# The up-projection of two MLPs by one level of Strassen's algorithm, in a two-block sequence model on one core

## The chip, the cores and the metric

The kernel runs on one core of one Trainium2 chip. The metric is the device time of the whole program in microseconds (us), and the figure compared is the median over runs. PE is TensorE's matmul, PEld its weight load, DVE VectorE, ACT ScalarE, POOL GpSimd and SP SyncE.

## The reference

Two layers of a hybrid block are followed by one layer of another block and a final norm, all float32, for 512 tokens of 1024 channels. The change touches only the MLP at the end of each first-block layer:

```python
def hybrid_layer(x, positions, norm_mix, w_in, conv_w, w_conv_out, ret_norm, w_ret_out, w_o,
                 norm_mlp, w_up, w_down):
    ...
    x = x + merged @ w_o
    h2 = rmsnorm(x, norm_mlp)
    return x + jnp.square(jax.nn.relu(h2 @ w_up)) @ w_down
```

`w_up` is 1024 x 4096 and `w_down` 4096 x 1024. The convolution, retention and gates ahead of `w_o`, and all of the second block (attention with selected and windowed keys, cross attention, gated MLP), keep their arithmetic.

## The kernel before

Activations lie channels by tokens: a tile has 128 channels on the partitions and 512 tokens, so `x` is eight tiles. Every float32 operand is written as the sum of two parts, hi and lo, that TensorE takes in one pass each, and a product is three matmuls: hi by hi, lo of the tokens by hi of the weights, hi of the tokens by lo of the weights (`mm3`, lines 233 to 235). An output tile of `w_up` or `w_o` is eight blocks of 128 x 128 weights, so 24 matmuls of 512 columns into one PSUM bank.

**The weight stream.** All weights lie in HBM as one array in the order of use. `_load` brings chunks of 16 blocks (1 MB, two buffers, SP queue). `_split` makes the parts of a unit of eight blocks: ACT rounds `raw` to `whi` (line 195), DVE subtracts to get `wlo` (line 196); three buffers of each. `block` hands out the next block and, at a unit's first block, asks for the split two units ahead.

**The order of the work.** A schedule written by hand sets the program order of every engine. `dense` runs the output tiles; the first G side by side up to a cut, so that late inputs are needed late. What follows an output tile (its evacuation) is a generator whose stages run at later ticks: `pulse` runs a stage of each once TensorE got `due` us of work since the last pulse, and then takes one step from the background list `bg`. `b1_norm_chain` puts two such steps there: the sum of squares over channels on PE (`norm_a`, line 340) with DVE and POOL making 1/rms of it (lines 343 and 345), and the broadcast over partitions (`bcast`, line 352) that ACT copies. Engines take their instructions in program order, each at its own pace.

**The MLP.** `ev_o` adds the output of `w_o` to `x` on DVE (line 561), makes the two parts of `x` times the norm's gain, and adds its squares to the running sum (`square_into`, ACT and, on POOL, line 363). The MLP is done in halves of 2048 hidden channels: 16 output tiles of `w_up`, each followed by relu (ACT), square (DVE), hi (ACT) and lo (DVE); then eight output tiles of `w_down` over 16 blocks each, scaled (DVE, line 589) and added to `x` (first half on POOL, line 594; second half on DVE, followed by the parts for the next layer).

```python
    def block(self, desc, n=1):
        ...
        self._split(u + AHEAD)
            a = [None] * 16
            ...
            self.dense(xm, [c8(f"w_up{i}", half * 2048, m) for m in range(16)], ev_up, G=1 if half else 2, cuts=[7])
            ...
            self.dense(a, [[(f"w_down{i}", half * 2048 + k * P, m * P) for k in range(16)] for m in range(KD)], ev_dn, G=2, cuts=[14])
```

Of the kernel before, what the change touches and what calls it, by code (L numbers as in the profile page):

```python
# [18 lines left out]
P = 128  # L19
S = 512  # L20
# [106 lines left out]
class Builder:  # L127
    def __init__(self, nc, tc, d, ccols, pcols, max_chunks):
        self.nc, self.tc, self.d = nc, tc, d
        self.ccols, self.pcols = ccols, pcols  # L130
        self.desc = []
        self.raw, self.whi, self.wlo = {}, {}, {}
        self.chunks = self.units = 0
        self.max_chunks = max_chunks
# [43 lines left out]
    def _load(self, c):  # L178
        while self.chunks <= min(c, self.max_chunks - 1):
            c0 = self.chunks  # L180
            t = self.wp.tile([P, CHUNK * P], F32, tag="raw", name=f"raw{c0}", bufs=2)
            self.nc.sync.dma_start(t, self.d["ws"][c0])
            self.raw[c0] = t
            self.chunks += 1

    def _split(self, u):
        last = self.max_chunks * (CHUNK // UNIT) - 1
        while self.units <= min(u, last):
            v = self.units
            c, h = divmod(v, CHUNK // UNIT)  # L190
            self._load(c + 2)
            raw = self.raw[c][:, h * UNIT * P:(h + 1) * UNIT * P]
            hi = self.wp.tile([P, UNIT * P], F32R, tag="whi", name=f"whi{v}", bufs=NW)
            lo = self.wp.tile([P, UNIT * P], F32R, tag="wlo", name=f"wlo{v}", bufs=NW)
            self.nc.scalar.activation(hi, raw, AF.Copy)  # L195
            self.nc.vector.tensor_sub(lo, raw, hi.bitcast(F32))  # L196
            self.whi[v], self.wlo[v] = hi, lo
            self.whi.pop(v - 8, None), self.wlo.pop(v - 8, None)
            self.units += 1

    def block(self, desc, n=1):
        """hi and lo of the next n blocks (adjacent in one unit); desc: one or a list."""
        ds = desc if n > 1 else [desc]
        i = len(self.desc)
        u, b = divmod(i, UNIT)
        assert b + n <= UNIT
        self._split(u + AHEAD)
        self.desc += ds
        return self.whi[u][:, b * P:(b + n) * P], self.wlo[u][:, b * P:(b + n) * P]

    def align(self):
        while len(self.desc) % UNIT:
# [1403 lines left out]
```

## Time and profile before

| | |
|---|---|
| runs, us | 2549.67, 2543.52, 2543.41 |
| median, us | 2543.52 |
| profiled execution, first to last instruction, us | 2547.5 |
| PE busy, us | 2523.5 (99%), 11,998 matmuls |
| weight load (PEld), us | 2102.5 (83%) |
| DVE, ACT, POOL busy, us | 1386.0 (54%), 911.7 (36%), 286.7 (11%) |
| mean granted clock | 0.994 |
| read from HBM | 232.15 MB, 92 GB/s |

No time of the profiled execution beside its span is on the page; the span lies between the runs. A matmul's duration holds its way through the array, and the next one starts before it ends: what a matmul costs in a stream is the distance between starts. Busy sums hold the same overlap.

### The profile page before, as it was taken

How to read it: one execution, taken by the hardware profiler on the slowest of the kernel's cores; microseconds unless marked ns; L12 is line 12 of the kernel's file. 1: busy time of each engine (PE TensorE's matmuls, PEld its weight loads, DVE VectorE, ACT ScalarE, POOL GpSimd, SP SyncE). 2: the span in 40 equal slices, each digit the busy share in tenths (PEclk: the TensorE clock that was granted, in tenths of full speed). 3: DMA queues.
4: the chain of work that ended last, by engine and by line, in shares of the span. 5: the costliest groups of instructions: out<-in, count | busy, mean ns of one | idle time of the engine just before them, and what ended most of it. 6: DMA issues, size and time to landing. Idle time of an engine off the chain costs nothing.

```text
span 2547.5 us, 29202 instructions
## 1 busy us (share of the span) xinstructions
PE 2523.5 (99%) x11998; PEld 2102.5 (83%) x11998; DVE 1386.0 (54%) x1902; ACT 911.7 (36%) x1416; POOL 286.7 (11%) x282
## 2 busy tenths in 40 slices
PE   8999999999999999999999999999999999999998
PEld 7888988888888888889888888888867888888886
DVE  6643645544344465356454434445679565683773
ACT  4232433333233322234333322333676444332221
POOL 2000100210100100011011000022100110220111
PEclk9999999999999999999999999999999999999999
DMA  4222222222222222222122222222200222222222
GB/s 177 107 99 100 73 77 86 97 99 100 100 91 94 97 100 99 100 83 83 68 98 99 99 99 87 96 98 103 102 32 34 101 84 96 85 100 100 99 85 81
DMA packets 34822, 236.13 MB, mean 93 GB/s; under 512 B 4032, under 2 KB 4032, under 8 KB 7040
## 3 DMA queue, kind: packets, MB, share of 16 engines
q1 hardware_dynamic: 33552, 231.90, 25.3%
q8 instruction: 94, 1.54, 0.2%
q0 software_dynamic: 416, 1.31, 0.2%
q10 hardware_dynamic: 720, 1.05, 0.1%
q14 instruction: 40, 0.33, 0.0%
HBM read 232.15 MB, written 2.10 MB: 92 GB/s over the span
## 4 chain that ended last, share of the span: by engine, by line
PE 96%; DVE 2%; ACT 1%; issue 1%; DMA 0%; POOL 0%; POOLq 0%; DVEq 0%; SPq 0%
PE mm L233 28%; PE mm L235 27%; PE mm L234 27%; PE nat L704 2%; PE nat L706 2%; PE nat L705 2%; PE oacc L1053 1%; PE ssq L340 1%; PE at L1042 1%; POOL ssq L363 0%; PE o L234 0%; PE o L235 0%; PE o L233 0%; PE bc L352 0%; DVE cv L228 0%
## 5 line engine op out<-in xcount | busy, mean ns | idle before, releaser
L233 PE MATMUL mm<-hi,whi 128*128 128x512 f32 x3040 | 1189.1, 391 | 6.9 <-ACT hi L225 6.9
L234 PE MATMUL mm<-lo,whi 128*128 128x512 f32 x3040 | 1184.8, 390 | 0.5 <-DVE lo L228 0.5
L235 PE MATMUL mm<-hi,wlo 128*128 128x512 f32 x3040 | 1184.8, 390 | 0.0
L196 DVE TENSOR_TENSOR wlo<-raw,whi 128x1024 fp32r<-128x1024 f32 x432 | 589.1, 1366 | 601.6 <-ACT whi L195 599.8
L233 PEld LDWEIGHTS mm<-hi,whi 128*128 128x128 f32 x3040 | 571.7, 188 | 123.7 <-ACT hi L225 6.9
L235 PEld LDWEIGHTS mm<-hi,wlo 128*128 128x128 f32 x3040 | 571.4, 188 | 119.3
L234 PEld LDWEIGHTS mm<-lo,whi 128*128 128x128 f32 x3040 | 571.7, 188 | 118.2 <-DVE lo L228 1.0
L195 ACT ACTIVATE whi<-raw 128x1024 fp32r<-128x1024 f32 x432 | 454.3, 1054 | 597.0 <-PE mm L234 541.2
L363 POOL TENSOR_TENSOR ssq<-ssq,sq 128x512 f32<-128x512 f32 x65 | 86.3, 1327 | 778.6 <-ACT sq L225 755.9
L225 ACT ACTIVATE up<-mm 128x512 f32<-128x512 f32 x64 | 38.0, 597 | 202.9 <-PE mm L235 202.9
L704 PE MATMUL nat<-whi,hi 128*128 128x256 f32 (+2 forms) x320 | 95.0, 297 | 0.0
L705 PE MATMUL nat<-wlo,hi 128*128 128x256 f32 (+2 forms) x320 | 94.2, 294 | 0.0
L706 PE MATMUL nat<-whi,lo 128*128 128x256 f32 (+2 forms) x320 | 94.2, 294 | 0.0
L225 ACT ACTIVATE hi<-x,par 128x512 fp32r<-128x512 f32 x48 | 34.1, 721 | 121.4 <-DVE x L561 47.1
L1479 POOL TENSOR_TENSOR fy<-fy,fy 128x512 f32<-128x512 f32 x22 | 44.6, 2028 | 250.9 <-DVE fy L228 242.5
L589 DVE TENSOR_TENSOR dn<-mm,rbc 128x512 f32<-128x512 f32 x32 | 22.1, 691 | 87.7 <-PE mm L235 87.7
L228 DVE SCALAR_TENSOR_TENSOR fy<-fz,par,fy 128x512 f32<-128x512 f32 x88 | 66.1, 752 | 6.1
L704 PEld LDWEIGHTS nat<-whi,hi 128*128 128x128 f32 x320 | 61.1, 191 | 1.4
L705 PEld LDWEIGHTS nat<-wlo,hi 128*128 128x128 f32 x320 | 61.1, 191 | 1.4
L706 PEld LDWEIGHTS nat<-whi,lo 128*128 128x128 f32 x320 | 61.1, 191 | 1.3
L628 POOL TENSOR_TENSOR ra<-ra,rb 128x512 f32<-128x512 f32 x16 | 27.5, 1721 | 291.6 <-DVE ra L627 281.3
L225 ACT ACTIVATE hi<-fy 128x512 fp32r<-128x512 f32 x22 | 13.9, 634 | 119.8 <-POOL fz L1468 107.5
(322 smaller groups left out, 2218.4 us busy)
## 6 DMA issues: line engine op xcount, KB each, us to landing
raw<-ws SPq DMA_DIRECT2D x215, 1024.0 KB, 4.8
x<-x SPq DMA_DIRECT2D x8, 256.0 KB, 5.6
raw<-ws SPq DMA_DIRECT2D x2, 512.0 KB, 5.2
dec<-dec SPq DMA_DIRECT2D x1, 1024.0 KB, 10.1
mem<-mem POOLq DMA_DIRECT2D x4, 256.0 KB, 4.6
y<-out ACTq DMA_DIRECT2D x4, 256.0 KB, 2.1
y<-out SPq DMA_DIRECT2D x4, 256.0 KB, 2.2
par<-par SPq DMA_DIRECT2D x1, 596.0 KB, 8.2
```

What stands on the lines that cost most here:

```text
L195: self.nc.scalar.activation(hi, raw, AF.Copy)
L196: self.nc.vector.tensor_sub(lo, raw, hi.bitcast(F32))
L225: self.nc.scalar.activation(out, in_, f, **kw)
L228: self.nc.vector.scalar_tensor_tensor(out, a, s, b, op0=op0, op1=op1, **kw)
L233: mm(out, w[0], x[0], start=start, stop=False, **kw)
L234: mm(out, w[0], x[1], start=False, stop=False, **kw)
L235: mm(out, w[1], x[0], start=False, stop=stop, **kw)
L363: self.nc.gpsimd.tensor_tensor(st["ssq"], st["ssq"], q, op=ALU.add)
L704: mm(p, xc[0], w[0][:, :n], start=k == 0, stop=False)
L705: mm(p, xc[0], w[1][:, :n], start=False, stop=False)
L706: mm(p, xc[1], w[0][:, :n], start=False, stop=k == K - 1)
L1479: nc.gpsimd.tensor_tensor(y, y, tmp["g"], op=ALU.mult)
```

## The change

**Products.** For two output tiles of `w_up` (a pair) the blocks are seen as four pairs of input tiles by two output tiles, and the tokens as two halves of 256. One level of Strassen's algorithm in Winograd's form makes the 2 x 2 x 2 product from seven products instead of eight. Each of the seven runs over four sums of weight blocks with 256 columns of token sums: 7 x 4 x 3 = 84 matmuls of 256 columns take the place of 48 of 512. They are numbered 1 to 7 in the code. Two PSUM banks per pair (`A`, `B`) hold sums that build up over the products, and copies of `A` between products take intermediate states to SBUF (`y1`, `y2`).

**Token sums.** `halves` makes, for each two tiles of `x`, four sums of 256 tokens on DVE and the hi and lo parts of seven operands: seven ACT and seven DVE instructions of 256 elements. It is a generator in four stages behind every second output tile of `w_o`.

**Weight sums.** Three of the seven weight operands (7, 5, 3) are a block row that a transfer loads plus one that a second transfer adds in place, issued from POOL (`accum_op`, 72 of these; 24 of 512 KB, 48 of 256 KB). Operands 6 and 3 get a further sum from a finished unit on DVE (`onto`: 24 of 1024 elements a partition, 16 of 512). 1 and 2 are plain.

**MLP in quarters.** A quarter is four pairs of `w_up` and then eight output tiles of `w_down` over eight blocks each. Pairs overlap: while the new pair runs products 1, 2, 7, 6, the old one runs 5, 3, 4. The first three quarters add into `x` on POOL, the last on DVE.

**Weight stream.** The unit of load is now the unit of split (up to 512 KB, six buffers); loads are asked for six units ahead, adding transfers four, splits two; four buffers of parts. There are 512 loads instead of 217 and 512 splits instead of 432.

How DVE's order moves at the start of the MLP of layer 0 (`x_91` and `x_94` are the last tile of `x`, `ms` the mean square from the sum of squares, `wlo` parts of weight units). Before:

```order
L561 TENSOR_TENSOR x_91<-mm_3973,x_91 128x512
L228 SCALAR_TENSOR_TENSOR lo_4004<-x_91,par,hi_4003 128x512
L196 TENSOR_TENSOR wlo_4014<-raw_3859,whi_4013 128x1024
L343 TENSOR_SCALAR ms_4047<-ssq_4042 128x4
L196 TENSOR_TENSOR wlo_4052<-raw_3859,whi_4051 128x1024
```

Now (`raw` added to `raw` is the further weight sum, `tu` and `tv` the token sums, `tf` the lo part of a token operand):

```order
L712 TENSOR_TENSOR x_94<-mm_4123,x_94 128x512
L224 TENSOR_TENSOR raw_3967<-raw_3967,raw_3928 128x512
L228 TENSOR_TENSOR wlo_4178<-raw_3967,whi_4177 128x512
L390 TENSOR_TENSOR tu_4199<-y_495_4165 128x256
L391 TENSOR_TENSOR tu_4199<-y_495_4165,y_496_4166 128x256
L392 TENSOR_TENSOR tv_4200<-tu_4199,y_495_4165 128x256
L393 TENSOR_TENSOR tv_4200<-tv_4200,y_496_4166 128x256
L498 TENSOR_SCALAR ms_4210<-ssq_4205 128x4
L228 TENSOR_TENSOR wlo_4218<-raw_4029,whi_4217 128x1024
L280 TENSOR_TENSOR tf_4230<-y_495_4165,tf_4230 128x256
```

`ms` stood behind one lo part and one weight unit; it now stands behind a weight sum, a weight unit and the four token sums, and the first token operand of the last two tiles behind `ms` and another weight unit. On PE the sum of squares stood 24 matmuls of 512 columns behind the last one of `w_o`; it now stands 18 matmuls of 256 columns behind it, and the broadcast another nine behind that.

How POOL's order moves where `w_down` ends and the next part of `w_up` begins, in layer 0 (`x` are tiles of the residual, `dn` a scaled output tile, `sq` squares). Before, first half to second half:

```order
L594 TENSOR_TENSOR x_83<-dn_4927,x_83 128x512
L594 TENSOR_TENSOR x_85<-dn_4989,x_85 128x512
L594 TENSOR_TENSOR x_89<-dn_5051,x_89 128x512
L594 TENSOR_TENSOR x_91<-dn_5113,x_91 128x512
L363 TENSOR_TENSOR ssq_5827<-ssq_5827,sq_5842 128x512
```

Now, first quarter to second quarter:

```order
L752 TENSOR_TENSOR x_84<-dn_4928,x_84 128x512
L213 DMA raw_4864<-wa 128x512
L752 TENSOR_TENSOR x_86<-dn_4963,x_86 128x512
L752 TENSOR_TENSOR x_92<-dn_4997,x_92 128x512
L752 TENSOR_TENSOR x_94<-dn_5031,x_94 128x512
L213 DMA raw_4967<-wa 128x1024
L213 DMA raw_5001<-wa 128x512
L213 DMA raw_5090<-wa 128x1024
```

The adding transfer of the unit that holds products 7 and 5 of the quarter's second step (`raw_4967`, 512 KB) stands behind the addition of the last output tile of `w_down`; nothing of POOL's was waited for there before.

The diff, cut to its core:

```diff
-CHUNK = 16
-AHEAD = 2
+H = S // 2
+LOAD, ACCUMULATE, SPLIT = 6, 4, 2
...
+    def sum_to(self, v):
...
+            more = self._known(u)["more"]
+            if more is not None:
+                at, n = more[0] * P, len(more[1]) * P
+                self.nc.gpsimd.dma_start(self.raw[u][:, at:at + n], self.d["wa"][self.more_at[u]][:, :n], accum_op=ALU.add)
...
+    def part_to(self, v):
...
+            if onto is not None:
+                self.nc.vector.tensor_tensor(raw[:, :n], raw[:, :n], self.raw[onto][:, :n], op=ALU.add)
...
+            self.nc.scalar.activation(hi[:, :n], raw[:, :n], AF.Copy)
+            self.nc.vector.tensor_sub(lo[:, :n], raw[:, :n], hi[:, :n].bitcast(F32))
...
+    def advance(self, u):
...
+        self.load_to(u + LOAD)
+        self.sum_to(u + ACCUMULATE)
+        self.part_to(u + SPLIT)
...
+    def halves(self, x1, x2, g1, g2):
...
+        self.act(y1, x1, AF.Copy, scale=g1)
+        self.act(y2, x2, AF.Copy, scale=g2)
+        yield
...
+        tt(u[:, :H], y1[:, :H], y1[:, H:], op=ALU.subtract)
+        tt(u[:, H:], y1[:, H:], y2[:, H:], op=ALU.subtract)
+        tt(v[:, :H], u[:, H:], y1[:, :H], op=ALU.subtract)
+        tt(v[:, H:], v[:, :H], y2[:, :H], op=ALU.add)
+        yield
...
+            self.act(out[f][:, :H], of[f])
+        yield
...
+            self.lo(out[f][:, H:], of[f], out[f][:, :H])
...
+    def strassen(self, X, pairs, done):
...
+            for k in ks or range(K):
+                w = slice((o + k) * P, (o + k + 1) * P)
+                while X[k] is None:
+                    self.tick(0.0)
+                self.mm3(p, (self.whi[u][:, w], self.wlo[u][:, w]), (X[k][f][:, :H], X[k][f][:, H:]),
+                         k == 0 and (f in (1, 2) or f == 4 and j in E), k == K - 1, skip_group_check=True)
+            self.tick(1.2)
...
+            xu = unit([(7, new), (5, old)])
+            yu = unit([(6, new), (3, old)], xu)
+            if old is not None:
+                unit([(4, old)])
+            if j == -1:
+                for f in (1, 2, 7):
+                    product(f, new, range(K - 1))
+                for f in (1, 2):
+                    product(f, new, [K - 1])
...
-            self.dense(xm, [c8(f"w_up{i}", half * 2048, m) for m in range(16)], ev_up, G=1 if half else 2, cuts=[7])
+            self.strassen(xm, [[c8(f"w_up{i}", (quarter * Q + 2 * j + e) * P, 0) for e in range(2)] for j in range(Q // 2)], up)
...
-            self.dense(a, [[(f"w_down{i}", half * 2048 + k * P, m * P) for k in range(16)] for m in range(KD)], ev_dn, G=2, cuts=[14])
+            self.dense(a, [[(f"w_down{i}", (quarter * Q + k) * P, m * P) for k in range(Q)] for m in range(KD)], ev_dn, G=3, cuts=[6])
...
-NW = 3
+NRAW = 6
+NW = 4
```

## Rows read from the trace of the kernel before

**Rows 1.** The page, parts 1 and 4: busy engines, and the chain that ended last

```profile
PE 2523.5 (99%) x11998; PEld 2102.5 (83%) x11998; DVE 1386.0 (54%) x1902; ACT 911.7 (36%) x1416; POOL 286.7 (11%) x282
...
PE 96%; DVE 2%; ACT 1%; issue 1%; DMA 0%; POOL 0%; POOLq 0%; DVEq 0%; SPq 0%
```

**Rows 2.** Stretches (MLP of layer 0, attention): busy us per engine (instructions), clock, DMA, GB/s

```profile
529.00:878.00 349.00, 349.00 (x1544) 289.07 (x1544) 149.65 (x161) 110.00 (x146) 21.57 (x16) 1.00 0.27 97
...
1845.00:1990.00 145.00, 139.62 (x806) 101.54 (x806) 118.82 (x283) 101.08 (x264) 11.74 (x13) 0.94 0.11 40
```

**Rows 3.** Timeline of DVE in `w_up`: start us, us, engine, line, operation, tiles

```profile
754.70 1.23 DVE L196 TENSOR_TENSOR wlo<-raw,whi 128x1024 fp32r<-128x1024 f32 x1 [3.01 <-ACT whi L195]
755.85 0.68 DVE L238 TENSOR_TENSOR lo<-up,hi 128x512 fp32r<-128x512 f32 x1
...
760.14 1.23 DVE L196 TENSOR_TENSOR wlo<-raw,whi 128x1024 fp32r<-128x1024 f32 x1 [3.01 <-ACT whi L195]
```

**Rows 4.** Timeline of PE in a retention head: products of 256 and of 128 columns

```profile
296.07 0.28 PE L705 MATMUL nat<-wlo,hi 128*128 128x256 f32 x1
...
299.07 0.28 PE L706 MATMUL nat<-whi,lo 128*128 128x256 f32 x1
...
306.58 0.28 PE L234 MATMUL sc<-lo,hi 128*128 128x128 f32 x1
306.69 0.27 PE L235 MATMUL sc<-hi,lo 128*128 128x128 f32 x1
```

**Rows 5.** Timeline of all engines where the MLP of layer 0 begins

```profile
523.02 0.39 PE L233 MATMUL mm<-hi,whi 128*128 128x512 f32 x1
523.22 0.69 DVE L561 TENSOR_TENSOR x<-mm,x 128x512 f32<-128x512 f32 x1 [0.96 <-PE mm L235]
...
528.46 0.95 PE L340 MATMUL ssq<-ones,ssq 128*128 128x1 f32 x8
...
529.44 0.16 DVE L343 TENSOR_SCALAR ms<-ssq 128x4 f32<-128x4 f32 x1 [1.74 <-PE ssq L340]
...
529.68 2.00 POOL L345 TENSOR_TENSOR rstd<-ms,mhalf 128x4 f32<-128x4 f32 x1 [3.06 <-DVE ms L343]
...
534.85 0.60 PE L352 MATMUL bc<-con,rstd 128*128 128x128 f32 x4
535.49 0.60 ACT L225 ACTIVATE rbc<-bc 128x512 f32<-128x512 f32 x1 [5.94 <-PE bc L352]
```

**Rows 6.** Groups by line and shape, whole program: busy us, mean ns, idle before

```profile
L225 ACT ACTIVATE sq<-x 128x512 f32<-128x512 f32 x56 | 34.1, 618 | 24.9 <-DVE x L1488 24.9
L225 ACT ACTIVATE hi<-x,par 128x512 fp32r<-128x512 f32 x48 | 34.1, 721 | 121.4 <-DVE x L561 47.1 <-DVE x L591 42.5 <-DVE x L1447 18.3
...
L225 ACT ACTIVATE kmh<-km 128x256 fp32r<-128x256 f32 x8 | 3.3, 406 | 0.0
...
L238 DVE TENSOR_TENSOR kml<-km,kmh 128x256 fp32r<-128x256 f32 x8 | 3.3, 416 | 0.0
...
L594 POOL TENSOR_TENSOR x<-dn,x 128x512 f32<-128x512 f32 x16 | 20.7, 1292 | 317.7 <-DVE dn L589 317.5
```

**Rows 7.** Timeline of ACT in `w_up`: a weight unit rounded

```profile
753.62 1.05 ACT L195 ACTIVATE whi<-raw 128x1024 fp32r<-128x1024 f32 x1
```

**Rows 8.** The tile mem: four transfers of 256 KB issued from POOL (min/median/max)

```profile
L1265 POOL DMA_DIRECT2D mem<-mem x4: 722/724/791, 1840.9 to 1843.2; - x4
...
DMA to landing us min/median/max: 3.1/4.6/7.8
```

**Rows 9.** The page, part 6: transfers, KB each, median us to landing

```profile
raw<-ws SPq DMA_DIRECT2D x215, 1024.0 KB, 4.8
...
dec<-dec SPq DMA_DIRECT2D x1, 1024.0 KB, 10.1
```

**Rows 10.** Stretches ahead of and in a fall of the clock, columns as in rows 2

```profile
1850.00:1854.00 4.00, 2.76 (x14) 1.66 (x14) 2.35 (x8) 4.00 (x13) 0.00 (x0) 1.00 0.68 283
...
1857.30:1864.10 6.80, 6.80 (x24) 4.80 (x24) 3.76 (x11) 4.23 (x12) 0.71 (x1) 0.50 0.01 2
```

More of the change, by code (lines that the diff above doesn't have):

```diff
@@ L175, in ps, with unit @@
         return self.pp.tile([P, S], F32, tag="ps", name=self.name(what), bufs=8)
[L178 to L199, printed above, removed]
+    def unit(self, blocks, more=None, onto=None):
+        self.units.append({"blocks": list(blocks), "more": more, "onto": onto})
+        return len(self.units) - 1
@@ new lines, in _known, with _last, load_to @@
+    def _known(self, v):
+        return self.plan[v] if self.plan is not None else {"blocks": [None] * UNIT, "more": None, "onto": None}
+    def _last(self):
+        return MOST - 1 if self.plan is None else len(self.plan) - 1
+    def load_to(self, v):
+        while self.loaded <= min(v, self._last()):
+            u = self.loaded
+            n = len(self._known(u)["blocks"]) * P
+            t = self.wp.tile([P, UNIT * P], F32, tag="raw", name=f"raw{u}", bufs=NRAW)
+            self.nc.sync.dma_start(t[:, :n], self.d["ws"][u][:, :n])
+            self.raw[u] = t
+            self.loaded += 1
@@ L201, in block @@
+    def advance(self, u):
+        for w in (self.whi, self.wlo):
+            for v in [v for v in w if v < u - 1 and v != self.cur]:
+                del w[v]
+        self.load_to(u + LOAD)
+        self.sum_to(u + ACCUMULATE)
+        self.part_to(u + SPLIT)
     def block(self, desc, n=1):
         ds = desc if n > 1 else [desc]
-        i = len(self.desc)
-        u, b = divmod(i, UNIT)
+        if self.cur is None or len(self.units[self.cur]["blocks"]) == UNIT:
+            self.cur = self.unit([])
+            self.advance(self.cur)
+        u = self.cur
+        b = len(self.units[u]["blocks"])
@@ L589, in ev_dn @@
                 tt(t, p, self.rbc2, op=ALU.mult)
-                if half:
+                if last:
                     tt(self.x[m], t, self.x[m], op=ALU.add)
@@ L1541 @@
 NPAD = 4
-NW = 3
+NRAW = 6
+NW = 4
+MOST = 600
 def weight_matrices(a):
@@ L1563, in weight_matrices, with pack_weights @@
     return w
[L1566 removed]
+def pack_weights(a, plan):
     w = weight_matrices(a)
[L1568 to L1576 removed]
+    more = [u["more"][1] for u in plan if u["more"] is not None]
+    out = []
+    for units in ([u["blocks"] for u in plan], more):
+        z = np.zeros((max(len(units), 1), P, UNIT, P), np.float32)
+        for n, blocks in enumerate(units):
+            for i, e in enumerate(blocks):
+                if e is not None:
+                    m, r, c = e
+                    z[n, :, i] = w[m][r:r + P, c:c + P]
+        out.append(z.reshape(-1, P, UNIT * P))
+    return out
 def make(a):
```

174 lines of the change are left out of this document (129 added, 45 removed).

## The prediction

> **What bounds the kernel now.** I read the busy line and the chain that ended last first. PE is busy 2523.5 of 2547.5 us, and the chain is PE for 96% of it [rows 1]: only PE's own work, or a hole in it, moves the end. The stretch table then says whether that holds where the change lies. In the MLP of layer 0 PE is busy for all of 349 us at full clock, while DVE has 150 us of work, ACT 110 and POOL 22, and the loads take 0.27 of the DMA engines at 97 GB/s [rows 2]. So time can be won there by fewer PE columns alone, and everything else has room, on average. The attention stretch keeps what holes there are, and the change does not touch it.
>
> A stream of matmuls is read by its starts. Two lo parts of successive weight units, each standing in the same place of its output tile of 24 matmuls, lie 760.14 − 754.70 = 5.44 us apart [rows 3], so a product of 512 columns costs 5.44/24 = 0.227 us. Products of 256 columns start 25 steps apart at 296.07 and 299.07 [rows 4]: 0.120 us each, more than half of 0.227. Each has its own load of 128 weight columns, as the new ones will.
>
> **Products.** A pair of output tiles falls from 48 x 0.227 = 10.88 us to 84 x 0.120 = 10.08 us. With 16 pairs a layer that is 0.8 x 16 = 12.8 us, for two layers **−25.6 us**. It is small since Strassen's seventh part less (12.5%) is half eaten by the dearer column; at 0.1295 us a product nothing would be left. The Trainium skill, TensorE: Matmul & The Clock Gate, section Back-to-back issue gap, gives a spacing at full clock of N/2.4 + 2.5 ns, so 216 and 109 ns here; by it the gain would be 38 us. The trace has 227 and 120, each about 11 ns more, and I keep the measured ones.
>
> **Start of an MLP (twice).** At present the last product of `w_o` starts at 523.02, DVE adds the tile from 523.22, and the sum of squares starts on PE at 528.46; `ms` follows at 529.44, 1/rms takes POOL from 529.68 for 2.00, and the broadcast starts at 534.85, all behind other products, so that PE does not stop [rows 5]. Now PE has 27 products of 256 columns there, 3.2 us, and two short matmul groups: 4.5 us in all. The chain needs, from the last `w_o` product: DVE add to 0.9, square on ACT (0.62) to 1.5, the running sum on POOL (1.29, as its other additions of this shape) to 3.0 [rows 6], PE's sum of squares (0.95) to about 3.9. Then DVE must finish `ms`, which stands behind a weight sum, the lo part of a unit (1.23) and four token sums of 256 (0.42 each, pitch lower): 5.6. 1/rms ends at 7.7 and the broadcast at 8.2, where PE has work to about 4.4: a hole of 3.8, and 0.5 for the copy of `A` behind `rbc` (0.60). 4.3 x 2 = **+8.6 us**; bounds 3 and 5 each, by how much of `ms`'s queue is done early.
>
> **Start of a further quarter (six).** PE does products 1, 2, 7, 6 of the first pair and 1, 2 of the second, 6 x 12 x 0.120 = 8.64 us after the last product of `w_down`; then it wants product 5, whose weights are the sum that POOL issues behind the last `x` addition. That addition needs DVE's scaled tile (0.2 to 1.0) and takes 1.29 [rows 6], so the transfer is issued at 2.33. From its landing, ACT needs 1.05 for the hi part [rows 7], DVE 1.23 for the lo part, of which two products (0.24) may run ahead, and two handovers: 2.1. With a time L from issue to landing, PE is stopped for 2.33 + L + 2.1 − 8.64 us, so nothing up to **L = 4.2**. No adding transfer is in the trace. The lower bound is the quickest POOL-issued 256 KB transfer, 3.1 (issue alone 0.72; median 4.6, longest 7.8) [rows 8]; the upper 10.1, the slowest 1 MB load [rows 9]. An add of 512 KB has to read the target as well, so it moves as much as a 1 MB load of the stream, landing in 4.8 [rows 9]; with POOL's 0.72 I take 5.5. The hole is 1.3, and 0.6 for the unit that adds this one to itself on DVE (512 elements 0.68) behind it. 1.9 x 6 = **+11.3 us**; bounds 0 and (2.33 + 10.1 + 2.1 − 8.64) + 0.6 = 6.5 each, 39.
>
> **End of a quarter (eight).** The last small unit (product 4) is split behind the last copy and relu: lo part at about 12.4 where PE is ready at 11.5, some 0.7 after what runs ahead: **+5.6 us**, bounds 0 and 8.
>
> **In between.** A step of one pair takes PE 10.08 us. DVE gets three whole lo parts and a weight sum at a pitch of 1.15 (754.70 to 755.85 [rows 3]), a half unit at half of it, three additions of 256 at 0.42 and three instructions of 512 at 0.68: 8.5 us. ACT gets three hi parts at 1.05 [rows 7] and a half, four copies of 256 at 0.41 and two hi parts of 512 at 0.62 [rows 6]: 6.6. The chain from product 3's end over the copy, two splits and the weight sum to the next unit fits with 0.1 to spare: **0**, bound 0.3 x 24 = 7. The DMA engines move 1.8 MB of loads and 0.8 MB of sums a step, 7.3 us at 97/0.27 = 359 GB/s [rows 2], 9.5 if a sum moves its bytes twice; below 10.08 either way. A load has six units, 15 us, for 4.8 + 5.5. The `x` additions of three quarters on POOL have a `w_down` tile's 5.4 us each and are hidden, as they are now; SP's more numerous issues are hidden by the same 15 us. Four instead of three part buffers and partial units elsewhere: 0 ± 3.
>
> **Sum.** −25.6 + 8.6 + 11.3 + 5.6 = −0.1 on the profiled span of 2547.5. The median of the runs, 2543.52, is 4.0 below that span, so 2543.4 on the runs; I say **2543.5**. A measurement of this kernel tells about 0.3% (7.6 us) from no change.
>
> **Rivals.**
> *B, the sums land in time.* L below 4.2, for which the quickest POOL-issued transfer, 3.1, and a median of 4.6 at half the size, close to the point, speak; against it that a sum reads its target. Then −25.6 + 8.6 + 5.6 = −11.4: 2532, and 2524 if the MLP's starts cost 3 and the ends nothing. The Trainium skill, DMA: Bandwidth & Descriptors, section Anatomy of one DMA — SWDGE (gpsimd) path, has 2.0 us plus the bytes at 436 GB/s for one transfer from GpSimd, an estimate of 3.2 us for 512 KB: by that rule this case holds. The trace's 3.1 at 256 KB is above the rule's 2.6, and its 4.6 far above.
> *A, the sums are late: slower.* The place is product 5 at a quarter's start, the point L = 4.2, and every us beyond costs six. At the 10.1 us of the one slow load it is 39 instead of 11.3, so 2571; and a step's load and sum then need 4.8 + 10.1 = 14.9 of the 15 us that six units give, so up to 0.3 to 1 us in each of 24 steps, to about 2590. For it: nothing on POOL's queue was waited for until now, and the transfers run beside twice as many loads. Against it: the DMA engines are idle for 0.73 of the MLP. The Trainium skill, Collectives: The Full Stack, section The bandwidth ceiling: the fold count and why AG ≠ RS ≠ AR, says that an adding transfer needs two source reads on one ring and has about half the rate (1.93); no run here shows it yet.
> *C, PE's clock falls in the new holes.* A stretch of 4 us with 2.76 busy was followed within 3.3 us by 6.8 us at half clock (0.50, 1.2 GHz) [rows 10], which costs 3.4 us. The holes at the MLP's starts are as long: two falls give 2550, a fall at all eight starts 2571. Against it: the holes of 4.3 us stand alone, between full streams.
> *D, the products don't hold 0.120* because operand order or bank changes differ from the retention heads. At 0.1295 the gain is gone: 2569. Products of 128 columns at 0.11 [rows 4] show that a load of 128 weight columns alone costs at most that, so I give it little.
>
> **How the numbers follow.** Forecast 0.40, with a range of its own of 2535 to 2553 (L 4.6 to 6.5, starts 3 to 5, the attention ± 3); B 0.25; A 0.20; C 0.11; D 0.04. Faster than 2535.9: most of B and the edge of the forecast, 0.26. Slower than 2551.1: A, D, half of C and the forecast's upper tenth, 0.34. Same: 0.40. The range 2522 to 2586 reaches from B with cheap ends to A with some cost in the steps, and leaves out about 0.12.
>
> **What would show it.** PE's products of 256 columns 0.120 apart, 1344 a layer; holes of about 4 us at the two MLP starts ended by `bcast`; holes of 1 to 3 us before product 5 at six quarter starts, with ACT's hi part waiting for the transfer of POOL; small ones before product 4 at the ends; no hole in between; clock 1.00 in the MLPs. The prediction is wrong if steps in the middle of a quarter have holes, if the sums land within 4.2 us or above 7, or if the clock falls.

## The result, and the profile after

| | before | after |
|---|---|---|
| median of the runs, us | 2545.47 (4 runs) | 2604.74 (4 runs) |
| ratio, 95% interval | | 1.0229 (1.0215 to 1.0244) |
| profiled span, us | 2547.5 | 2602.9 |
| mean granted clock | 0.994 | 0.986 |

The change makes the kernel 59 us slower; it now reads 281.96 MB from HBM instead of 232.15. The page after, parts 1, 4, 3 and 6, against [rows 1] and [rows 9]:

```profile
PE 2527.1 (97%) x13150; PEld 2154.5 (83%) x13150; DVE 1501.4 (58%) x2198; ACT 1015.8 (39%) x1680; POOL 437.4 (17%) x386
...
PE 79%; DVE 9%; ACT 6%; issue 3%; DMA 2%; POOL 1%; POOLq 0%; DVEq 0%; SPq 0%; ACTq 0%
...
q1 hardware_dynamic: 76032, 256.56, 29.3%
q0 software_dynamic: 10784, 26.48, 6.1%
...
raw<-ws SPq DMA_DIRECT2D x444, 512.0 KB, 3.4
raw<-wa POOLq DMA_DIRECT2D x48, 256.0 KB, 5.1
raw<-wa POOLq DMA_DIRECT2D x24, 512.0 KB, 5.6
```

PE was 96% of the chain and is 79%; the rest is now mostly other engines' work that PE waits for. The adding transfers (`wa`) land 5.6 us after issue at the median, nearly the 5.5 of the forecast. So the median is not where the error lies. The stretches of layer 0's first two quarters tell more (columns as in rows 2):

```profile
524.45:543.00 18.55, 13.10 (x73) 12.36 (x72) 13.07 (x26) 9.63 (x20) 7.85 (x7) 0.72 0.62 147
543.00:573.00 30.00, 30.00 (x252) 30.00 (x252) 21.10 (x30) 17.63 (x32) 3.40 (x4) 1.00 0.80 208
573.00:585.00 12.00, 10.65 (x58) 8.67 (x58) 10.20 (x16) 10.28 (x16) 0.00 (x0) 1.00 0.68 219
585.00:621.86 36.86, 36.86 (x165) 30.52 (x164) 11.75 (x14) 5.03 (x6) 13.86 (x8) 1.00 0.28 86
621.86:630.70 8.84, 8.84 (x74) 8.78 (x72) 3.44 (x4) 1.97 (x3) 3.37 (x3) 1.00 0.65 155
630.70:634.40 3.70, 0.25 (x4) 0.05 (x2) 0.30 (x1) 1.33 (x2) 0.79 (x1) 0.86 0.95 265
634.40:641.00 6.60, 6.41 (x31) 6.11 (x32) 5.17 (x7) 3.07 (x5) 0.92 (x2) 0.56 0.94 182
```

Inside a part PE is full: 30.00 of 30.00 us and 252 matmuls, 0.12 us each. Time is lost at the borders: in the MLP's first 18.55 us (13.10 busy, clock 0.72), at the quarter's end (573 to 585, 10.65 of 12), and at the next quarter's start, 3.70 us with 0.25 busy and then 6.60 us at a mean clock of 0.56. The DMA engines, at 0.27 in the MLP before, are at 0.62 to 0.95 while `w_up` runs.

Per place, from PE's starts: what a matmul's start lies later than 0.227 or 0.120 us after the one before it is a stop where it is over 0.28 us, and the clock's loss where it is less (products alone are counted, not the norm's short matmuls). All MLP parts of both layers:

| place | count | forecast, us | stops, us | clock's loss, us |
|---|---|---|---|---|
| products (2 x 1344 of 0.120 for 2 x 768 of 0.227) | | -25.6 | -25.6 | |
| start of an MLP | 2 | +8.6 | 6.1 + 6.4 = 12.5 | 5.0 |
| start of a further quarter | 6 | +11.3 | 24.4 (3.6 to 4.7 each) | 12.1 |
| end of a quarter | 8 | +5.6 | 15.1 (1.9 each) | 2.9 |
| between | | 0 | 0 | 0 |
| end of `w_down`'s last part | 2 | (other, 0 ± 3) | 0.74 + 6.83 = 7.6 | 0.4 |

The sum is −25.6 + 59.6 + 20.4 = +54.4, against 2602.9 − 2547.5 = 55.4 between the spans. The forecast had −0.1: the stops are 34.1 us more than it added up, and the clock's 20.4 were not in its sum.

**A quarter's start.** Timelines of POOL, ACT and PE there:

```profile
623.05 1.67 POOL L752 TENSOR_TENSOR x<-dn,x 128x512 f32<-128x512 f32 x1 [3.78 <-DVE dn L747]
624.67 1.74 POOL L213 DMA_DIRECT2D raw<-wa  x2
```

```profile
633.02 1.06 ACT L227 ACTIVATE whi<-raw 128x1024 fp32r<-128x1024 f32 x1 [6.70 <-DMA raw<-wa]
633.98 0.37 ACT L267 ACTIVATE y<-sa 128x256 f32<-128x256 f32 x1
```

```profile
630.67 0.28 PE L277 MATMUL sb<-tf,wlo 128*128 128x256 f32 x1
634.40 0.58 PE L275 MATMUL sa<-tf,whi 128*128 128x256 f32 x1 [3.45 <-ACT y L267]
```

The transfer goes out at 624.67, 2.6 us after `w_down`'s last product, as forecast (2.33). It lands at 632.9: ACT's hi part had waited 6.70 us for it, and the copy of `A` that PE needs stands behind that on ACT. L, the time from issue to landing, is 8.2 here and 7.6 to 8.7 at the six starts, not 5.5. The buffers of the next loads come free with the weight sum and the splits behind `w_down`'s last tile (DVE, up to 626.5), so three 512 KB loads, issued at 623.64, 625.30 and 626.56, and a second adding transfer go out within 2 us of the first; the DMA engines are at 0.95 while it is waited for.

**A quarter's end.** Timelines of ACT and PE before product 4 of the first quarter's last pair:

```profile
573.26 0.63 ACT L267 ACTIVATE y<-y 128x512 f32<-128x512 f32 x1 [1.09 <-DVE y L481]
573.79 0.61 ACT L227 ACTIVATE whi<-raw 128x512 fp32r<-128x512 f32 x1
```

```profile
574.46 0.38 PE L275 MATMUL se<-tf,whi 128*128 128x256 f32 x1 [0.89 <-ACT whi L227]
```

The hi part of product 4's unit stands on ACT behind a relu of the pair before, which waits for DVE. PE stops for 1.05 us, for 0.38 more behind two matmuls, where it waits for the lo part, and for 0.45 in `w_down`'s first blocks: 1.9 at each end, where the forecast had 0.7.

**An MLP's start.** Timelines of DVE and PE, at the place of [rows 5]:

```profile
523.38 0.68 DVE L712 TENSOR_TENSOR x<-mm,x 128x512 f32<-128x512 f32 x1
...
529.13 0.67 DVE L712 TENSOR_TENSOR x<-mm,x 128x512 f32<-128x512 f32 x1
...
534.45 0.15 DVE L498 TENSOR_SCALAR ms<-ssq 128x4 f32<-128x4 f32 x1
```

```profile
524.45 0.39 PE L277 MATMUL mm<-hi,wlo 128*128 128x512 f32 x1
...
531.93 0.37 PE L495 MATMUL ssq<-ones,ssq 128*128 128x1 f32 x1 [3.12 <-POOL ssq L518]
...
536.68 1.12 PE L507 MATMUL bc<-con,rstd 128*128 128x128 f32 x4 [0.75 <-POOL rstd L500]
```

DVE adds the last tile at 529.13, 4.7 us after the start of its last product; the forecast had 0.2. The sum of squares starts at 7.5 us instead of 3.0, the broadcast at 12.2 instead of 8.2. PE stops three times: 1.74 us for the lo part of a token operand from DVE, 3.28 for the running sum of squares from POOL and 1.04 for 1/rms.

**The end of layer 1.** Timelines of DVE and ACT in `w_down`'s last part, one tile:

```profile
1779.68 0.68 DVE L747 TENSOR_TENSOR dn<-mm,rbc 128x512 f32<-128x512 f32 x1
1780.39 0.69 DVE L749 TENSOR_TENSOR x<-dn,x 128x512 f32<-128x512 f32 x1
1781.88 0.75 DVE L270 SCALAR_TENSOR_TENSOR lo<-x,gp,hi 128x512 fp32r<-128x512 f32 x1 [0.79 <-ACT hi L267]
1783.96 2.17 DVE L228 TENSOR_TENSOR wlo<-raw,whi 128x1024 fp32r<-128x1024 f32 x1 [1.33 <-ACT whi L227]
1786.06 0.68 DVE L747 TENSOR_TENSOR dn<-mm,rbc 128x512 f32<-128x512 f32 x1
```

```profile
1781.12 0.72 ACT L267 ACTIVATE hi<-x,gp 128x512 fp32r<-128x512 f32 x1 [3.57 <-DVE x L749]
1781.75 0.61 ACT L267 ACTIVATE sq<-x 128x512 f32<-128x512 f32 x1
1782.27 0.71 ACT L267 ACTIVATE sqg<-x,par 128x512 f32<-128x512 f32 x1
1782.89 1.05 ACT L227 ACTIVATE whi<-raw 128x1024 fp32r<-128x1024 f32 x1
```

DVE and ACT wait for each other in a ring: addition, hi, two squares, the next unit's hi part, its lo part (2.17 us here; 1.22 at the median of the lo parts during which POOL is idle), the next tile. A turn takes 1786.06 − 1779.68 = 6.38 us, where PE needs 5.44 for a tile over eight blocks. Timeline of DVE before, in the same part:

```profile
1722.95 0.69 DVE L589 TENSOR_TENSOR dn<-mm,rbc 128x512 f32<-128x512 f32 x1 [3.16 <-PE mm L235]
...
1733.90 0.69 DVE L589 TENSOR_TENSOR dn<-mm,rbc 128x512 f32<-128x512 f32 x1 [3.23 <-PE mm L235]
...
1738.20 2.18 DVE L196 TENSOR_TENSOR wlo<-raw,whi 128x1024 fp32r<-128x1024 f32 x1 [1.33 <-ACT whi L195]
```

There a tile over sixteen blocks took 1733.90 − 1722.95 = 10.95 us. The same chain took 1738.20 + 2.18 − 1733.90 = 6.48 of them, and DVE waited for PE ahead of each tile: the ring had room.

### The profile page after: what moved, and what is told of

It reads as the page before. It is cut to its first block, busy times and chain, and to the rows that moved or that the text cites. A ratio compares the mean times of both kernels' runs of the same rounds, so it can differ in the third digit from the quotient of the medians.

```text
span 2602.9 us, 33187 instructions
## 1 busy us (share of the span) xinstructions
PE 2527.1 (97%) x13150; PEld 2154.5 (83%) x13150; DVE 1501.4 (58%) x2198; ACT 1015.8 (39%) x1680; POOL 437.4 (17%) x386
## 3 DMA queue, kind: packets, MB, share of 16 engines
q0 software_dynamic: 10784, 26.48, 6.1%
q10 hardware_dynamic: 720, 1.05, 0.1%
HBM read 281.96 MB, written 2.10 MB: 109 GB/s over the span
## 4 chain that ended last, share of the span: by engine, by line
PE 79%; DVE 9%; ACT 6%; issue 3%; DMA 2%; POOL 1%; POOLq 0%; DVEq 0%; SPq 0%; ACTq 0%
PE mm L276 20%; PE mm L275 20%; PE mm L277 20%; ACT whi L227 2%; DVE wlo L228 2%; DMA raw<-wa 2%; PE nat L862 2%; PE nat L863 2%; PE nat L864 2%; ACT y L267 1%; PE sa L277 1%; PE sa L275 1%; PE sa L276 1%; DVE cv L270 1%; PE sb L275 1%
## 5 line engine op out<-in xcount | busy, mean ns | idle before, releaser
L275 PE MATMUL mm<-hi,whi 128*128 128x512 f32 x2528 | 990.8, 392 | 6.2 <-ACT hi L267 6.2
L276 PE MATMUL mm<-lo,whi 128*128 128x512 f32 x2528 | 987.2, 391 | 2.4 <-DVE lo L280 1.8
L277 PE MATMUL mm<-hi,wlo 128*128 128x512 f32 x2528 | 986.6, 390 | 1.3 <-DVE wlo L228 1.3
L228 DVE TENSOR_TENSOR wlo<-raw,whi 128x1024 fp32r<-128x1024 f32 (+2 forms) x512 | 611.0, 1201 | 400.3 <-ACT whi L227 396.1
L227 ACT ACTIVATE whi<-raw 128x1024 fp32r<-128x1024 f32 (+2 forms) x512 | 501.8, 996 | 467.8 <-PE mm L276 268.7
L275 PE MATMUL sa<-tf,whi 128*128 128x256 f32 x512 | 149.5, 292 | 20.1 <-ACT y L267 20.1
L277 PE MATMUL sa<-tf,wlo 128*128 128x256 f32 x512 | 149.0, 291 | 2.3 <-DVE wlo L228 2.3
L276 PE MATMUL sa<-tf,whi 128*128 128x256 f32 x512 | 147.9, 289 | 3.2 <-DVE tf L280 3.2
L275 PEld LDWEIGHTS sa<-tf,whi 128*128 128x128 f32 x512 | 101.2, 198 | 22.0 <-ACT y L267 21.5
L276 PEld LDWEIGHTS sa<-tf,whi 128*128 128x128 f32 x512 | 101.3, 198 | 3.9 <-DVE tf L280 3.6
L275 PE MATMUL sb<-tf,whi 128*128 128x256 f32 x352 | 103.6, 294 | 0.0
L276 PE MATMUL sb<-tf,whi 128*128 128x256 f32 x352 | 103.0, 293 | 0.0
L277 PE MATMUL sb<-tf,wlo 128*128 128x256 f32 x352 | 102.7, 292 | 0.0
```

The lines of the kernel that those rows point to most:

```text
L227: self.nc.scalar.activation(hi[:, :n], raw[:, :n], AF.Copy)
L228: self.nc.vector.tensor_sub(lo[:, :n], raw[:, :n], hi[:, :n].bitcast(F32))
L275: mm(out, w[0], x[0], start=start, stop=False, **kw)
L276: mm(out, w[0], x[1], start=False, stop=False, **kw)
L277: mm(out, w[1], x[0], start=False, stop=stop, **kw)
```

## The experiments

Each kernel was timed against the one before on the same chip; the medians of before lie from 2545.0 to 2547.1. "After" is the changed kernel.

### What holds the sum at a quarter's start

**The last `x` addition on DVE.**

```diff
                 if last:
...
+                elif m == KD - 1:
+                    tt(self.x[m], t, self.x[m], op=ALU.add)
                 else:
```

> Theory Q (POOL's queue): at the six later quarter starts the addition of the last output tile of w_down to x stands on POOL ahead of the adding transfer; with that one addition on DVE the transfer goes out when its load has landed, some 5 us earlier, and while the DMA engines are idle. The six holes of 3.6 to 4.7 us shrink to under 0.7 each (together 24.4 to under 4) and the clock no longer falls there (another 12 us): span about 2567. Rival T (the adding transfers themselves are late, because the DMA engines are full at a quarter's start): the holes stay above 2.5 us and the span above 2590.

2581.57, ratio 1.0145 (1.013 to 1.016): 23 us won by one moved instruction in six places. Timeline of POOL and ACT at the same border:

```profile
616.52 1.66 POOL L754 TENSOR_TENSOR x<-dn,x 128x512 f32<-128x512 f32 x1 [3.23 <-DVE dn L747]
618.12 1.76 POOL L213 DMA_DIRECT2D raw<-wa  x2
```

```profile
625.12 1.05 ACT L227 ACTIVATE whi<-raw 128x1024 fp32r<-128x1024 f32 x1
```

The transfer leaves 3 us before `w_down` ends, with the second sum but no load beside it, and lands after 5.29 us (5.2 to 5.5 at the six starts); the hi part waits for nothing. The six stops before product 5, 24.4 us, are gone, and the clock no longer falls there, so POOL's queue is the cause of them. But 7.9 us of stops come up one step later, where there were none, and the stops before product 4 grow at three ends, from 1.05 to 1.1, 1.5 and 1.9. So 13 us less are won than theory Q had. Stretches of this kernel (columns as above):

```profile
621.00:630.00 9.00, 9.00 (x76) 8.98 (x75) 6.52 (x8) 4.58 (x8) 0.78 (x1) 1.00 0.94 251
630.00:641.00 11.00, 11.00 (x94) 11.00 (x94) 6.10 (x9) 4.17 (x7) 0.93 (x2) 1.00 0.89 235
641.00:660.00 19.00, 18.00 (x146) 17.45 (x145) 14.89 (x22) 12.46 (x23) 3.44 (x4) 1.00 0.81 206
```

The DMA engines run at 0.81 to 0.94. That they are why what started late is not caught up is argued from these shares, not shown.

**All `x` additions on DVE.**

```diff
+                tt(self.x[m], t, self.x[m], op=ALU.add)
                 if last:
-                    tt(self.x[m], t, self.x[m], op=ALU.add)
                     self.next_norm(i, m)
-                else:
-                    nc.gpsimd.tensor_tensor(self.x[m], t, self.x[m], op=ALU.add)
```

> All additions of w_down's tiles to x on DVE, so POOL has nothing ahead of the adding transfers in w_down. With the last one alone moved the time was 2581.6, and holes of 7.9 us at the quarter starts and 4.6 in the next steps were left. Theory M (what is left is the DMA engines' own time, 0.88 to 0.94 busy there because an adding transfer takes about twice a load's time): little changes, 2577 to 2584. Rival Q2 (POOL's other additions still hold transfers back): the six starts go under 0.7 us each and the time to 2572.

2583.1, ratio 1.0137 (1.012 to 1.0154): no gain over moving the last one, as theory M had it. No stop is left at the starts; 7.8 us of them stand in the steps behind, and the stops before product 4 are up to 2.2 us long. So POOL's other additions are not what holds the sums; that the DMA engines' time is, this run does not show.

**The second transfers without the addition** (the weight sums are left out).

```diff
-                self.nc.gpsimd.dma_start(self.raw[u][:, at:at + n], self.d["wa"][self.more_at[u]][:, :n], accum_op=ALU.add)
+                self.nc.gpsimd.dma_start(self.raw[u][:, at:at + n], self.d["wa"][self.more_at[u]][:, :n])
```

> The 72 second transfers overwrite instead of adding, so the weight sums are left out; everything else stays. Theory Q with the sum's double traffic: the transfer at a quarter's start lands in 6 instead of 8.3 us, the six holes fall from 4.1 to about 2 and the clock's loss there by a third: span about 2586. Rival T': the landing is set by waiting behind loads and on POOL alone and not by the add: holes of 4 as before, span 2603.

2591.39, ratio 1.0178 (1.0161 to 1.0195); the starts' stops fall from 24.4 to 17.2, between theory Q's 12 and the rival's 24. At the border shown above the transfer lands after 6.2 us instead of 8.2, so the addition is a part of its lateness and not all. Part 3 of this kernel's page, and its transfers in part 6:

```profile
q0 software_dynamic: 7712, 26.48, 3.2%
...
raw<-wa POOLq DMA_DIRECT2D x24, 512.0 KB, 3.8
```

The same 26.48 MB take 3.2% of the DMA engines' time as plain writes and 6.1% as additions: an addition costs them 1.9 times a plain transfer. The Trainium skill, Collectives: The Full Stack, section The bandwidth ceiling: the fold count and why AG ≠ RS ≠ AR, has 1.93 between an AllGather, which copies, and a ReduceScatter, whose addition reads two sources; the trace agrees. An adding transfer also takes POOL longer to issue (0.91 us at the mean, 0.55 plain).

**Adding transfers five units ahead.**

```diff
-LOAD, ACCUMULATE, SPLIT = 6, 4, 2
+LOAD, ACCUMULATE, SPLIT = 6, 5, 2
```

> The kernel of the change with one number altered: adding transfers are asked for five units ahead and not four. On POOL the transfer that product 5 waits for now stands one place earlier: ahead of the last x addition at a quarter's start and ahead of the last running sum of squares at an MLP's start. Theory Q (POOL's order): as much is won at the six quarter starts as by moving the addition to DVE, 23 us, and a second hole at the MLP's start doesn't come: about 2581. Rival M (the transfer is late since the DMA engines are full): under 8 us, above 2596.

2594.26, ratio 1.0178 (1.0161 to 1.0195), between the two theories. At the six starts the stops fall to 7.1, as theory Q has it, but five of the stops before product 4 grow from 1.05 us to between 2.2 and 3.7, each with half clock behind it, and 1.7 us come up within the steps. There POOL waits with an adding transfer for its load, and the DMA engines are at 0.81 to 0.86. So the order on POOL makes the hole at the border. That the DMA engines' load decides how much of it comes back is argued: no run had both the order mended and the load taken off.

### The MLP's start

**The norm four products later.**

```diff
-        self.bg = first + [a, b] +
+        self.bg = first + [lambda: None] * late + [a, b] +
...
-        self.b1_norm_chain(st, sq=True)
+        self.b1_norm_chain(st, sq=True, late=4)
```

> The sum of squares and the broadcast at the start of each MLP come four products later on PE. Theory N (the norm's chain makes the hole): the holes of 3.3 and 1.0 us of each start go, and with them most of the clock's fall there: span about 2588. Rival S (the token operands of the last two tiles of x are late, behind DVE's backlog, since DVE adds the last tile only 4.7 us after its product): PE then waits for these operands instead, in one hole of 6 to 7 us at each start, and the span stays within 4 us of 2603.

2612.95, ratio 1.0264 (1.0249 to 1.028): 8 us slower still, which neither theory had. PE waits for the last tiles' token operands instead, as rival S has it, but the stops of the two starts grow from 12.5 to 17.6 us (timeline of PE):

```profile
528.61 0.39 PE L276 MATMUL sa<-tf,whi 128*128 128x256 f32 x1 [1.58 <-DVE tf L280]
...
534.88 0.38 PE L275 MATMUL sa<-tf,whi 128*128 128x256 f32 x1 [3.61 <-ACT tf L267]
...
537.41 0.58 PE L276 MATMUL sa<-tf,whi 128*128 128x256 f32 x1 [2.15 <-DVE tf L280]
```

So behind the norm, on which the forecast set this term, stands a chain that ends later still.

**Stages every two blocks in `w_o`.**

```diff
-        self.due = 1.5
+        self.due = 1.2
```

> One number: in w_o a stage of what follows is issued every two blocks and not every third (due 1.2 for 1.5), so that the seven lo parts of the tiles before come ahead of the last tile but one instead of ahead of the last tile. Theory S (the MLP's start is late by DVE's backlog ahead of the last tile's addition, 4 us): that addition comes within 1.5 us of its product, the holes of 6.1 and 6.4 us fall to 3 or less each, the clock's loss with them: about 2594. Rival (DVE and ACT are simply full in w_o, so the backlog only changes its order): holes of 5 or more, 2601 to 2606.

2605.98, ratio 1.0229 (1.0212 to 1.0246): the rival. The stops are 6.0 and 6.5, and the last addition still comes 4 us late: the backlog was only put in another order.

**The ring in `w_o` taken apart** (square one stage behind the addition; operands 1, 2, 7 before the others; due 1.2; norm later).

```diff
...
             tt(self.x[m], p, self.x[m], op=ALU.add)
+            if m < KD - 1:
+                yield
             self.square_into(st, self.x[m])
...
```

> Only the MLP's start changes: operands 1, 2 and 7 of each two tiles of x are made first and the other four after them; the square of a tile comes one stage behind its addition; due 1.2; the sum of squares and the broadcast four steps later each. Theory S (the start waits for DVE's and ACT's ring: addition, square, weight unit's hi part, its lo part, next addition): the last tile is added within 2 us of its product and operands 1 and 2 are ready some 3 us after it; the holes of 6.1 and 6.4 us go to under 2.5 each and the clock doesn't fall there: 2604.7 - 14 = about 2591. Rival (DVE is full in w_o, so order doesn't help): holes of 5 or more, above 2600.

2608.98, ratio 1.0247 (1.0232 to 1.0262). The last addition now follows its product at once, but the stops are still 5.1 and 5.4, with 4.5 of clock each: theory S had under 2.5, and the numbers are the rival's, though not for its cause. With the backlog gone, what is left is the chain from the addition over square, two scalings and a weight unit to the first operands. Timeline of PE:

```profile
529.68 0.38 PE L276 MATMUL sa<-tf,whi 128*128 128x256 f32 x1 [2.19 <-DVE tf L280]
...
531.82 0.58 PE L276 MATMUL sb<-tf,whi 128*128 128x256 f32 x1 [1.16 <-DVE tf L280]
```

### Ends, and the last part

**One stage between the last quarter's addition and its parts.**

```diff
                     tt(self.x[m], t, self.x[m], op=ALU.add)
+                    if m < KD - 1:
+                        yield
                     self.next_norm(i, m)
```

> In the last quarter the parts and squares of the new x come one stage later than the addition, behind the next weight unit's split. Theory D: each w_down tile of the last quarter of layer 1 runs as one ring DVE, ACT, DVE of 6.38 us against PE's 5.44; taken apart, the holes of 0.8, 0.8 and 5.3 us at the end of layer 1 shrink to under 1 together: span about 2596. Rival: POOL's two running sums of squares a tile (1.3 us each) are what comes last; the holes stay and the span is 2603.

2595.66, ratio 1.0195 (1.018 to 1.0211): 9 us won, and no stop is left in either layer's last part. The ring was the cause.

**Product 4's parts one product earlier.**

```diff
                 if new is not None:
+                    if new + 1 == n:
+                        self.part_to(at[4, old][0] + 3)
                     product(4, old)
```

> The parts of the last small unit of a quarter (product 4) are asked for one product earlier, so that they stand ahead of the evacuation of the pair before on ACT and DVE. Theory E (order on ACT: the hi part waited 1.0 us behind a relu that waited for DVE): the 1.05 + 0.39 us holes of all eight quarter ends go, with 0.3 of clock: 8 x 1.4 to 1.8, so 2604.7 falls to about 2592. Rival (the evacuation that is put back then delays w_down's first tile): the later hole of 0.45 grows to 1.5 and the time stays above 2600.

2609.3, ratio 1.0242 (1.0227 to 1.0257): nothing won. The stop before product 4 went, and others of 0.5 to 0.65 came before product 3 and in `w_down`'s first blocks.

**The whole end:** that, each copy of `A` ahead of the evacuation before it, and four blocks first in `w_down`.

```diff
+            if then is not None:
+                self.act(*then)
             self.tick(1.2)
...
-                product(3, old)
-                self.act(Y[old][0][:, H:], A[old][:, :H])
+                product(3, old, then=(Y[old][0][:, H:], A[old][:, :H]))
...
-            self.dense(a, ..., ev_dn, G=3, cuts=[6])
+            self.dense(a, ..., ev_dn, G=3, cuts=[4, 6])
```

> Only the quarter's end changes: product 4's parts one product earlier, each copy of A issued ahead of the evacuation of the pair before, and w_down's first three tiles begin with four blocks instead of six. Theory C (a chain on ACT and DVE from the last products over copy, relu, square, parts to w_down's blocks 4 to 7; moving one link of it moved the hole): with the copy first and 4 us later need the ends cost under 0.5 instead of 2.3 us each: 2604.7 - 14 = about 2591. Rival (the chain is as long as the work that covers it in any order): 1.5 or more each, above 2598.

2599.23, ratio 1.0204 (1.0187 to 1.0221): the ends fall from 1.9 to 0.7 us each, 0.2 above what theory C had, and the time by 5.5. Which of the three edits did it is open; the clock's losses at the starts came out larger in the profiled run, 21.5 for 17.0.

### The parts alone, and everything together

**Quarters in the kernel before,** with plain products and its own weight stream.

```diff
-        for half in range(2):
-            a = [None] * 16
+        for quarter in range(4):
+            a, last = [None] * 8, quarter == 3
...
-            self.dense(a, ..., ev_dn, G=2, cuts=[14])
+            self.dense(a, ..., ev_dn, G=3, cuts=[6])
```

> The kernel before with its MLP in quarters and nothing else: eight plain output tiles of w_up, then eight of w_down over eight blocks (first three tiles together up to block 6). Theory P (what costs time is what Strassen's products need at the part borders, not the smaller parts): only the ring in layer 1's last part is new, 7 us, and quarter borders stay closed: 2545 + 7 = about 2552. Rival H (smaller parts alone open the borders, since each begins and ends a chain): 2 us and more at each of eight ends, 2562 or above.

2560.19, ratio 1.0051 (1.0035 to 1.0068). In the MLPs there is no stop at any border between parts, which is against rival H; 0.8 and 7.2 us are in the layers' last parts, where theory P had them. P's time was 8 us too low. Some 3 of that are the clock's, the rest stays open: behind 5.20 us with one matmul the clock was at 1.2 GHz for 6.6 (stretches of this kernel):

```profile
1745.20:1750.40 5.20, 0.10 (x1) 0.00 (x0) 3.20 (x4) 2.61 (x4) 1.30 (x2) 0.83 0.55 192
1750.40:1757.00 6.60, 6.51 (x23) 5.90 (x24) 2.86 (x6) 1.13 (x2) 5.91 (x11) 0.50 0.21 50
```

So 14 of the 59 us come with the quarters alone, and 45 with Strassen's products and their weight stream on top of them.

**Everything together** came in steps. First the edits of additions on DVE, the stage in the last part, product 4's parts, due 1.2:

> All of it: additions on DVE, the last quarter taken apart by one stage, product 4's parts earlier, due 1.2. If the causes are apart from each other their effects add: 2604.7 - 23 - 9 - 12 - 10 = about 2551, still slower than before (2545) by a little. If they share a cause (the DMA engines' time above all), less is won: 2560 or more.

2570.47, ratio 1.0093 (1.0078 to 1.0108). The expected 2551 counted gains of 10 and 12 for due and the earlier parts, which alone gave none; here they gave 3.6 at most, against the single gains of the other two (2604.7 − 21.6 − 9.1 = 2574.0).

Then additions on DVE, the stage in the last part, the whole end and `w_o`'s ring taken apart:

> All together: additions on DVE, the last quarter taken apart by a stage, and both changes of this call. By the trace of the four together before (2570.5; starts of the MLPs 17.7 us with the clock's part, ends 19, quarter starts 6) with 14 and 14 less: about 2542, level with before (2547). If the product count's 25 us came out in full: 2522. If ends or starts stay as they were: 2556 or more.

2563.4, ratio 1.007 (1.0052 to 1.0088): the MLP's starts kept 4.6 and 7.2 us. By their single gains the four edits would come to 2604.7 − 21.6 − 9.1 − 5.5 + 4.2 = 2572.7, so some of them pay more where others are in place.

To this, a tile scaled right behind its addition, and operands 1, 2, 7, 6 first:

```diff
...
+            ys[m] = y = self.slot(what="y")
+            self.act(y, self.x[m], AF.Copy, scale=self.prm(f"mlp{i}", m))
+            t = self.slot(S, True, "tf")
+            self.act(t[:, :H], y[:, :H])
+            if m < KD - 1:
+                self.square_into(st, self.x[m])
+                yield
+            self.lo(t[:, H:], y[:, :H], t[:, :H])
+            xm[m // 2][1 + m % 2] = t
...
```

> All changes of the last call, and at the MLP's start the last two tiles' operands by the shortest chain: each tile is scaled right behind its addition, its square after that, operands 1, 2, 7 and 6 ahead of any weight unit's parts. Theory S2 (the start's hole is the chain of dependent steps on the last tile: addition 0.7, square 0.6, two scalings 1.3, hi 0.4, a weight sum and a weight unit's lo part 1.4, lo 0.4, against 3.2 us of PE work; the backlog was only part of it): operands 1 and 2 come 2.5 us after the product, the holes of 4.6 and 7.2 us fall to 1.5 or less and the clock stays up: 2563 - 13 = about 2550. Rival (the weight units of the first step are what PE waits for there, as POOL's sums for them land late): holes of 4 or more, 2560 or above.

2569.22, ratio 1.009 (1.0075 to 1.0105). The operands 1 and 2 of the last tile were ready 2.6 us after its product, as theory S2 said, and no product waited for them; but the stop moved on to ACT's copy of `A`, behind the later operands and a weight unit (timeline of PE):

```profile
531.35 0.58 PE L275 MATMUL sa<-tf,whi 128*128 128x256 f32 x1 [4.72 <-ACT y L267]
```

POOL's 1/rms, waiting 12 us for the late norm, held the next sums, and a second stop of 4.2 followed.

The kernel of 2563.4 with transfers five units ahead:

> e11_all with the adding transfers five units ahead. The quarter starts are nearly closed there (under 1 us but for one of 2.2), so by Theory Q only the MLP's starts can win, where the sum stands behind the last running sum of squares: 2563 - 4 = about 2559, and no change (2563) if the tokens' operands are what comes last there.

2553.93, ratio 1.0029 (1.0017 to 1.0041): 9 us won, more than the 4 expected; the MLP's starts stop PE for 4.4 and 4.6, and the second stop there is gone.

And the kernel of 2569.2, mended where its trace had PE wait, also with five units:

```diff
...
-                    product(f, new, range(K - 1))
-                for f in (1, 2):
-                    product(f, new, [K - 1])
-                self.act(Y[new][0][:, :H], A[new][:, :H])
-                product(7, new, [K - 1])
+                    product(f, new, range(K - 1), tick=False)
+                product(1, new, [K - 1], then=(Y[new][0][:, :H], A[new][:, :H]), tick=False)
+                product(2, new, [K - 1], tick=False)
+                product(7, new, [K - 1], tick=False)
...
```

> e13_start2 mended in three places: the first copy of A stands right behind its product on ACT and ahead of the later token operands; no stages are issued between the first products; the norm is two steps late instead of four, and transfers are asked for five units ahead, so that POOL isn't held by 1/rms when the first sums are due. Theory S3 (three waits in series stood at the MLP's start: the backlog, the chain on the last tile, then ACT's copy and POOL's order): the two starts cost under 4 us each with the clock's part instead of 14, so 2569 - 20 = about 2549. Rival (weights of the first step land too late in any order): 8 or more each, above 2558.

2549.56, ratio 1.0017 (1.0002 to 1.0032): the time of the theory of waits in series. The starts stop PE for 3.5 and 4.4 us, which with the clock's part is over the 4 that it had for each, and the rest is spread: eight ends of 0.7 to 1.7, six quarter starts of 0.4 to 2.7. This takes back 55 of the 59 us and is 4 us behind the kernel before: no version found here beats it.

## Why the prediction was wrong

The forecast was 2543.5, no change, and its widest range ended at 2586; 2604.74 was measured. Two of its own signs of being wrong came: the sums landed above 7 us at the quarter starts, and the clock fell.

- **The bound, and the products: right.** PE's columns were the limit; 225 starts from 545.09 to 571.97 lie 0.120 us apart, there is no stop inside a part, and the gain of 25.6 came in full. The Trainium skill's 109 ns (TensorE: Matmul & The Clock Gate, Back-to-back issue gap), which the section gives for a single matmul alone, was too short by 11 ns here as well.
- **L = 5.5 at a quarter's start: the step that failed.** Place and issue time were right, and so was the sum around L: with the measured 7.6 to 8.7 it gives 4.0 to 5.1 us a start, 27.0 in all, where 24.4 were measured. Right was even 5.5, for a transfer with no load beside it: 5.2 to 5.5 in the first experiment. But held back behind the last `x` addition, the sum starts together with the loads whose buffers come free there and a second sum: 24.4 us in place of 11.3. Rival A named the loads beside it; its L of 10.1, and so its 39 us, were too high.
- **Rival C was likelier than its 0.11, and each fall cheaper than its 3.4 us.** The clock fell at all eight starts. Each such stop is a stretch nearly without matmuls (0.25 us busy in 3.70), and what followed ran at 1.2 GHz: 17.0 us together, where C had 27 for eight falls. It was no case of its own, but came with the stops, on top of the forecast's and A's terms alike, and where the stops went (first experiment) it went. How long a stop may be is not read from these runs: the stops of 1.05 us at the ends had no half clock behind them, but one of 1.9 us in the first experiment had, and one of 2.0 us with the stage in the last quarter had not.
- **The start of an MLP: the chain was wrong in two places,** 12.5 us for 8.6. It was counted from an idle DVE, "add to 0.9" behind the product; DVE came 4 us late out of `w_o`. And behind the norm stood a longer chain, the last tile's operands, that had no term: with the backlog gone the stops were still 10.5 us. (The row at 523.02 is also not the last product of `w_o`: by the 24 products up to the sum of squares at 528.46 it is the first of `w_up`, 0.2 us later.)
- **Quarter ends: undersized,** 15.1 for 5.6, above the bound of 8: 1.43 in place of 0.7 around product 4, whose hi part waits on ACT behind a relu that waits for DVE, and 0.45 in `w_down`'s first blocks, which had no term.
- **"Other, 0 ± 3": wrong by 7.6.** Halving the depth of `w_down`'s tiles halves the time that covers their evacuation: the ring of 6.4 us had been in the trace of before, inside tiles of 10.95.
- **Rival B** (the sums land in time, the rule of the Trainium skill's DMA: Bandwidth & Descriptors, Anatomy of one DMA — SWDGE (gpsimd) path) fell: an estimate of 3.2 us by the rule, 3.8 measured at the median for plain transfers of this size, 5.6 for adding ones.

## What to carry to other kernels

A smaller multiplication count pays inside a part; the price is paid at its borders, where each operand that has to be made (token sums, weight sums, copies) adds a link to a chain that PE must wait for. So count the borders, and at each one start the chain from the engine's real backlog, not from idle, and take a transfer's time from what starts beside it, not from a median. And when parts are halved, look for rings that were hidden because a part was longer than the ring.

## What was not expected of the hardware

At the six quarter starts, half the granted clock behind the stops (1.2 GHz for 3.4 or 6.8 us) cost 12.1 us on top of 24.4. An adding transfer took 1.9 times the DMA engines' time of a plain one (6.1% against 3.2% for 26.48 MB) and 0.91 instead of 0.55 us of POOL to issue. An adding transfer of 512 KB landed 5.2 to 5.5 us after its issue with no load beside it, and 7.6 to 8.7 with three loads and a second one started within 2 us.
